# A four-layer decoder trunk: longer runs of equally wide matmuls, and attention scores with both low terms of a head in one product

## The chip, the cores and the metric

The kernel runs on one core of a Trainium2 chip. The metric is the device time of one execution in microseconds. In the profile PE is the matrix engine (TensorE) and PEld its weight loads, DVE is VectorE, ACT is ScalarE, POOL is GpSimd and SP is the engine that issues most transfers.

## The reference

The trunk has four layers over one stream h of 256 tokens with 1024 features, all in float32. Layers 0 and 3 mix tokens with differential attention, layer 1 with MoBA attention (one block of 256 at this length, so plain causal attention), layer 2 with sliding-window attention with sinks. After each mixer comes a squared-ReLU MLP with 4096 hidden features.

```python
for i in range(DEPTH):
    a = rms_norm(h, attn_norm_g[i])
    y = ...                      # by i % 3: diff_attention, moba_attention, swa_sink_attention
    h = h + y
    h = h + sqrelu_mlp(rms_norm(h, mlp_norm_g[i]), mlp_w_up[i], mlp_w_down[i])
return rms_norm(h, final_norm_g)

# in each mixer: q and k get a partial rotary turn, then
s = jnp.einsum('bqhcd,bkhcd->bhcqk', qi, k)      # diff: two components c for each of 8 heads
p = softmax(where(causal, s, -inf)); p = p[:, :, 0] - lam * p[:, :, 1]
o = jnp.einsum('bhqk,bkhe->bqhe', p, v)

def sqrelu_mlp(h, w_up, w_down):
    a = jnp.maximum(h @ w_up, 0)
    return (a * a) @ w_down
```

A head of queries or keys is 64 wide.

## The kernel before

**Two parts of each operand.** Float32 operands of the large products are split in a high part, rounded to the type fp32r, and a low part, the rest. A product is the sum of three: high by high, high by low and low by high. Weights come in pieces of 128 x 2048 elements (1 MB): one transfer to `raw`, then ACT writes `whi` and DVE writes `wlo` as `raw - whi`, half a piece (1024 columns) at a time. There are four buffers of `raw` and three each of `whi` and `wlo`; PE's last product on a piece frees its buffers.

**Stages of a layer.** Input projection (`proj`, accumulator `p_in`), mixer, output projection (`out_proj`, `p_d`), up projection (`up_proj`, `p_up`, 16 groups g of one piece each), down projection (`down_proj`, `p_down`, 16 pieces: two, h = 0 and 1, for each of 8 blocks d; in the last layer `down_out` with `p_last`). The activations are stored as `[..., (high, low), 256]`, so in up and down a product with a high weight takes both parts at once (512 columns, `part` 0) and one with a low weight takes the high part alone (256 columns, `part` 1). `block_step` issues one such product. In `up_proj` the order before is: block b of 128 output features, then part, then the 8 steps k over features; runs of eight 512-wide and eight 256-wide products alternate. The first group runs k outermost, since the normed inputs (`hg`, class `Normed`) become ready one after another. In `down_proj` the order is part, then 16 steps k.

The result of a group of up goes through `joined` (ACT copies the second half to `cross`, DVE adds it to the first), `squared` (tile `u`), `high` and `low` (tile `uu`).

**Scores.** `turn` transposes the queries or keys of two blocks on PE into a bank (`p_qk`). A block is two heads of 64 that stand one above the other on the 128 rows. `Queries` writes high and low to a tile `qhl`; `put_keys` writes the high part of the keys to `kpadh` and the low part to `kpadl`. The key tiles have an extra axis h of two: for h = 0 only rows 0 to 63 are filled, for h = 1 only rows 64 to 127, and the other rows hold zeros (`Keys.clear`, memsets on POOL), so one product with all 128 rows gives both heads side by side. `scores` does for each of two row tiles t of 128 queries three products (`mm3`): 256 wide for t = 0 and 512 wide for t = 1. `least` (DVE), `exp` (ACT), the division, `turned` (transposes `p_t`) and the values' products (`p_av`) follow, then the transposes `p_o` in layers 0 and 3, and the tile `oo`, which `p_d` reads. The mixer of layers 0, 1 and 3 has four groups of two blocks, that of layer 2 has 8 blocks too.

**Order of the work.** Everything is a task of a `Plan` with an engine, a cost in microseconds, the tasks before it, and buffers that it takes. The plan is run through as a simulation with those costs, and each engine's instructions are then issued in the order of the simulated start times and kept in that order (class `Ordered`). PE has a main sequence of weight products, and the tasks of the attention are put between them as soon as their inputs are due. The plan reserves for a score block 1.05 us of PE. Some tasks have a second engine that the plan may choose. All instructions go through one helper, so the profile shows line 191 for nearly all of them; tiles tell them apart.

Of the kernel before, what the change touches and what calls it, by code (L numbers as in the profile page):

```python
# [18 lines left out]
P = 128  # L19
# [15 lines left out]
LESS = 2.0  # L35
WAY = 0.6
MARGIN = 56


def f(ap):  # L40
# [157 lines left out]
def trunk(ctx: ExitStack, tc: tile.TileContext, xT, gains, lams, swa_row, fng, weights, out):  # L198
# [44 lines left out]
    def pe(cost, do, after=(), rank=1, **kw):  # L243
        return add("PE", cost, do, after, lag=0.3, rank=rank, **kw)
# [339 lines left out]

    COLS = (slice(1, 1 + P), slice(1 + P, 1 + 3 * P))

    def scores(q, k, mask, sinks, sums_of, after, begin=None):

        st = {}

        def products():
            st["p"] = [bank("p_s0"), bank("p_s1", 1)]
            (qh, ql), (kh, kl) = q(), k()
            for t, n in ((0, P), (1, S)):
                o = st["p"][t][:, :2 * n].rearrange("p (h m) -> p h m", h=2)
                a = slice(P * t, P * t + P)
                mm3(o, qh[:, a], ql[:, a], kh[:, :, :n], kl[:, :, :n], True, True)

        first = pe(1.05, products, after, take={"wk": 2, "e": 1})
# [46 lines left out]

    class Keys:

        def __init__(self, after):
            self.tiles = []  # L650

            def clear():
                for x in range(2):
                    t = room(10 + x, [P, 2, 2, S], f"kpad{'hl'[x]}", F32R)
                    self.tiles.append(t)
                    for h in range(2):
                        G.memset(f(t[HD * (1 - h):HD * (1 - h) + HD, :, h, :]), 0.0)

            self.clear = add("POOL", 2.2, clear, after)

    def turn(src, n, after):

# [10 lines left out]

    class Queries:

        def __init__(self, src, after):
            p, a = turn(src, 2, after)
            self.both = None

            def high():  # L680
                self.both = room(plan.now.got["q"][0], [P, 2, 2, S], "qhl", F32R)
                A.activation(self.both[:, 0], p(), AF.Copy, scale=0.125)

            def low():
                V.scalar_tensor_tensor(self.both[:, 1], p(), 0.125, f(self.both[:, 0]), op0=OP.mult, op1=OP.subtract)

            self.hi = act(512, high, [a], take={"q": 1})
            self.lo = dve(512, low, [self.hi])
            give("wk", [self.lo], a)

        def of(self, b):
            return lambda: [self.both[:, x, b] for x in range(2)]

    def put_keys(keys, src, n, after):

        p, a = turn(src, n, [keys.clear, *after])
        halves = [slice(HD * h, HD * h + HD) for h in range(2)]

        def high():
            for h, s in enumerate(halves):  # L700
                A.activation(keys.tiles[0][s, :n, h, :], p()[s], AF.Copy)

        def low():
            for h, s in enumerate(halves):
                V.tensor_tensor(keys.tiles[1][s, :n, h, :], p()[s], f(keys.tiles[0][s, :n, h, :]), op=OP.subtract)
# [4 lines left out]
        return lo  # L710

    class Diff:

# [3 lines left out]
        def head(self, h, q, k, after):  # L717
# [7 lines left out]
            st, exps, first = scores(q, k, causal, None, lambda c: l1[0] if c else self.l0[g][:, h % 2], after, begin)  # L725

            def combine():
                c2 = tiny.tile([P, NT], F32, tag="c2", name="c2")
# [84 lines left out]
    class Heads:  # L813
# [4 lines left out]
        def head(self, b, q, k, after):  # L818
# [2 lines left out]
            def begin():  # L821
                st2["l"] = tiny.tile([P, 2, NT], F32, tag="l", name="l", bufs=6)

            st, exps, first = scores(q, k, self.mask, self.sinks and self.sinks(b), lambda c: st2["l"][:, c], after, begin)
            ends, a = [], None
            for c in range(2):

# [59 lines left out]
    def mixer_layer(i, n):  # L887
        mixer, slot = i % 3, i // 3
        r = n.factor(False) if i else None
        keys = Keys([main[0]])  # L890
        if mixer == 2:
            return windowed(n, r, keys)
        v, vr, qk, queries, firsts = [], [], {}, [], []
# [2 lines left out]
        for at, c in enumerate((0, 1, "v", 2, 3, "v")):  # L896
# [14 lines left out]
            if c == "v":  # L911
                v.append(to)
                vr.append(got)
            else:
                if i == 0 and at == 0:
                    made["rope"] = rotary_tables()
                    made["lam"] = lambdas(pieces[-1].hi[-1].after[0])
                a = roped(to, 8, [*got, made["rope"]])
                queries.append(Queries(lambda j, t, to=to: to[0][:, t, P * j:P * j + P], [a]))
                k = put_keys(keys, lambda j, t, to=to: to[0][:, t, P * (2 + j):P * (2 + j) + P], 2, [a, *firsts[-2:]])  # L920
                for b in range(2):
                    h = 2 * c + b
                    firsts.append(heads.head(h, queries[c].of(b), lambda b=b: [x[:, b] for x in keys.tiles],
                                             [queries[c].lo, k]))
# [8 lines left out]
    def windowed(n, r, keys):  # L933
# [24 lines left out]
        for c, (width, other, pairs) in enumerate(((512, S, (0,)), (256, 0, (1,)), (512, 0, (2, 3)))):  # L958
# [17 lines left out]
            if c == 0:  # L976
                k = put_keys(keys, lambda j, t: st[0][:, t, P:2 * P], 1, [a])
            for g in pairs:
                q = Queries(lambda j, t, c=c, at=other + S * (g - pairs[0]): st[c][:, t, at + P * j:at + P * j + P], [a])
                for b in range(2):  # L980
                    firsts.append(heads.head(2 * g + b, q.of(b), lambda: [x[:, 0] for x in keys.tiles],
                                             [q.lo, k, negated]))
# [5 lines left out]

    def block_step(p, w, x, part, start, stop):
        if part:  # L990
            matmul(p[:, :S], w, x[:, 0], False, stop)
        else:
            matmul(r3(2)(p), w, x, start, False)

    def joined(o, p, after):

# [41 lines left out]
    def up_proj(n, then):  # L1038

        us = []  # L1040
        for g in range(16):
            w = piece()
            st = {}
            order = [(b, part, k) for b in range(2) for part in range(2) for k in range(8)]
            if g == 0:
                order.sort(key=lambda x: x[2])
            for at, (b, part, k) in enumerate(order):

                def do(b=b, part=part, k=k, w=w, st=st):
                    if not st:  # L1050
                        st["p"] = two_banks("p_up")
                    block_step(st["p"][:, b], w.at(part, 8, k)[:, P * b:P * b + P], n.both[k // 2][:, k % 2], part,
                               k == 0, k == 7)
# [9 lines left out]
            a = joined(sum_to, lambda st=st: st["p"], [t])  # L1063
            give("acc", [a], begin)

            def squared(st=st):
                st["u"] = sb.tile([P, 512], F32, tag="u", name="u")
# [16 lines left out]
    def down_proj(us, n, row):  # L1084
# [20 lines left out]
        for d in range(8):  # L1105
            if d % 2 == 0:
                st = {}
            for h in range(2):
                w = piece()
                for part, k in ((part, k) for part in range(2) for k in range(16)):  # L1110

                    def do(d=d, h=h, k=k, part=part, w=w, st=st):
                        if not st:
                            st["p"] = two_banks("p_down")
                        block_step(st["p"][:, d % 2], w.at(part, 16, k), us[16 * h + k][1](), part,
                                   h + k == 0, h == 1 and k == 15)
# [244 lines left out]
```

## Time and profile before

| | |
|---|---|
| median of 3 runs | 1142.52 us (1142.29 to 1143.0) |
| the profiled execution | 1142.88 us, its span 1141.1 us |
| instructions | 16569 |
| PE busy | 1128.6 us (99%) |
| DVE / ACT / POOL busy | 814.4 / 650.1 / 42.3 us |
| mean granted clock of TensorE | 0.997 |

The page gives busy times by engine, then the span in 40 slices, the queues, the chain of work that ended last, and groups of instructions. A matmul's busy time in the groups is that of one instruction from start to its modelled end, and neighbours overlap; the cost of one in a stream is read from the distance between starts, or from a stretch of the chain divided by its count.

### The profile page before, as it was taken

The page shows a single profiled execution, that of the slowest core. Times are in us where ns is not written, and L with a number is a line of the kernel's source. Part 1 is how long each engine was busy: PE and PEld are TensorE (multiplying, and loading weights), DVE is VectorE, ACT ScalarE, POOL GpSimd, SP SyncE. Part 2 cuts the span into 40 slices and gives each one's busy share as a digit, 9 for nine tenths or more (in the row PEclk, how much of TensorE's full clock was granted, in tenths as well). Part 3 has the DMA queues.
Part 4 walks back from the last instruction along what each step waited for, and adds up shares of the span by engine and source line. Part 5 has one row for each costly group of instructions (what it writes and reads, how often), then busy time and mean ns, then how long its engine had stood idle before and what let it go on. Part 6 is the DMA issues. An engine that isn't in the chain of part 4 may idle for free.

```text
span 1141.1 us, 16569 instructions
## 1 busy us (share of the span) xinstructions
PE 1128.6 (99%) x6462; PEld 983.4 (86%) x6462; DVE 814.4 (71%) x1385; ACT 650.1 (57%) x1126; POOL 42.3 (4%) x71
## 2 busy tenths in 40 slices
PE   8999999999999999999999999999999999999997
PEld 7889888888888898888887888888888899888886
DVE  8887887656676779775568799775568777877453
ACT  7877655444487665554446775544446776555342
POOL 1000000000100000000011000000010000100000
PEclk9999999999999999999999999999999999999999
DMA  8544555555444455555554175555544445555541
GB/s 305 186 148 147 213 194 185 185 185 188 159 144 160 139 198 194 188 184 185 186 176 141 39 257 186 184 185 187 188 159 169 148 143 179 196 184 203 185 147 37
DMA packets 30031, 198.65 MB, mean 174 GB/s; under 512 B 3456, under 2 KB 4864, under 8 KB 6528
## 3 DMA queue, kind: packets, MB, share of 16 engines
q1 hardware_dynamic: 29664, 197.19, 50.0%
q8 instruction: 51, 0.84, 0.3%
q10 hardware_dynamic: 288, 0.39, 0.1%
q14 instruction: 28, 0.23, 0.1%
HBM read 196.52 MB, written 1.05 MB: 173 GB/s over the span
## 4 chain that ended last, share of the span: by engine, by line
PE 98%; DVE 1%; issue 0%; DMA 0%; ACT 0%; POOLq 0%; POOL 0%; DVEq 0%
PE p_up L191 31%; PE p_down L191 23%; PE p_in L191 20%; PE p_d L191 8%; PE p_last L191 7%; PE p_s L191 3%; PE p_av L191 2%; PE p_t L191 1%; PE p_qk L191 1%; PE p_o L191 0%; DVE qn L191 0%; DMA gn<-in_gains 0%; DVE turns L191 0%; PE p_res L191 0%; DVE an L191 0%
## 5 line engine op out<-in xcount | busy, mean ns | idle before, releaser
L191 DVE TENSOR_TENSOR wlo<-raw,whi 128x1024 fp32r<-128x1024 f32 (+1 forms) x374 | 443.5, 1218 | 207.8 <-ACT whi L191 194.5
L191 ACT ACTIVATE whi<-raw 128x1024 fp32r<-128x1024 f32 (+1 forms) x374 | 374.2, 1042 | 320.2 <-issue 102.0
L191 PE MATMUL p_up<-hg,whi 128*128 128x512 f32 x1024 | 263.2, 393 | 0.0
L191 PEld LDWEIGHTS p_up<-hg,whi 128*128 128x128 f32 x1024 | 184.7, 189 | 33.8
L191 PE MATMUL p_in<-whi,hg 128*128 128x512 f32 (+1 forms) x672 | 187.2, 391 | 1.6 <-DVE hg L191 1.4
L191 PE MATMUL p_down<-uu,whi 128*128 128x512 f32 x768 | 183.2, 391 | 0.0
L191 PEld LDWEIGHTS p_down<-uu,whi 128*128 128x128 f32 x768 | 141.1, 188 | 27.3
L191 PE MATMUL p_up<-hg,wlo 128*128 128x256 f32 x1024 | 151.9, 282 | 0.0
L191 PEld LDWEIGHTS p_up<-hg,wlo 128*128 128x128 f32 x1024 | 143.1, 190 | 9.4
L191 PEld LDWEIGHTS p_in<-whi,hg 128*128 128x128 f32 x672 | 121.9, 188 | 25.5 <-DVE hg L191 1.8
L191 PE MATMUL p_in<-wlo,hg 128*128 128x512 f32 (+1 forms) x336 | 105.8, 390 | 0.4 <-DVE wlo L191 0.4
L191 PEld LDWEIGHTS p_down<-uu,wlo 128*128 128x128 f32 x768 | 98.5, 191 | 3.7
L191 PE MATMUL p_down<-uu,wlo 128*128 128x256 f32 x768 | 99.6, 283 | 0.0
L191 PE MATMUL p_d<-oo,whi 128*128 128x256 f32 x512 | 96.3, 289 | 0.0
L191 PEld LDWEIGHTS p_d<-oo,whi 128*128 128x128 f32 x512 | 80.0, 192 | 1.3 <-issue 1.1
L191 PE MATMUL p_last<-whi,uu 128*128 128x512 f32 x256 | 78.9, 389 | 0.0
L191 PEld LDWEIGHTS p_in<-wlo,hg 128*128 128x128 f32 x336 | 62.0, 188 | 13.0 <-DVE wlo L191 0.8
L191 PE MATMUL p_d<-oo,wlo 128*128 128x256 f32 x256 | 72.6, 284 | 0.0
L191 ACT ACTIVATE e<-ns,nm 128x128 f32<-128x128 f32 (+3 forms) x128 | 57.0, 449 | 14.8 <-DVE nm L191 14.1
L191 PEld LDWEIGHTS p_last<-whi,uu 128*128 128x128 f32 x256 | 48.1, 188 | 9.9
L191 ACT ACTIVATE uu<-u 128x512 fp32r<-128x512 f32 x64 | 40.0, 625 | 27.8 <-DVE u L191 27.8
L191 DVE TENSOR_TENSOR relu<-p_up,cross 128x512 f32<-128x512 f32 x64 | 43.9, 686 | 10.7 <-ACT cross L191 10.7
(155 smaller groups left out, 1000.6 us busy)
## 6 DMA issues: line engine op xcount, KB each, us to landing
raw<-in_weights SPq DMA_DIRECT2D x183, 1024.0 KB, 4.9
raw<-in_weights SPq DMA_DIRECT2D x8, 256.0 KB, 4.7
hT<-in_xT SPq DMA_DIRECT2D x8, 128.0 KB, 4.5
out<-last SPq DMA_DIRECT2D x2, 320.0 KB, 2.3
bias<-in_swa_row SPq DMA_DIRECT2D x1, 512.0 KB, 5.8
grow<-in_fng SPq DMA_DIRECT2D x1, 512.0 KB, 3.7
out<-last ACTq DMA_DIRECT2D x2, 192.0 KB, 2.3
lv<-in_lams SPq DMA_DIRECT2D x1, 256.0 KB, 7.8
```

The source lines that it names most:

```text
L191: x = getattr(self.engine, name)(*args, **kw)
```

## The change

Two things are changed.

1. Order in the MLP. `up_proj` runs both blocks b of a part before it changes the part, even groups with part 0 first and odd groups with part 1 first; the first group goes by two halves of four steps k. `down_proj` runs the second piece of each block d with part 1 first. The flags that start and end an accumulation follow. The tile `u` becomes two tiles, `u0` and `u1`, used in turn.

2. Scores of layers 0, 1 and 3 (`both` is true). The product of high queries and high keys stays as it is. For the two low terms, there is one tile for the queries (`qhl`) that holds, for head c, the low queries on the rows of head c and the high queries on the other 64 rows, and one tile for the keys (`kboth`) that holds for head c the high keys on the rows of head c and the low keys on the other rows. One product over 128 rows, for one head, then gives low by high and high by low at once: 128 or 256 columns wide, and two of them (c = 0, 1) for a row tile. The high queries now stand in a tile in the slots of `u0` and `u1`. The high parts on the other rows are copies between halves of the rows: a task `copied` of two instructions, with ACT as its engine and POOL as its second. The low queries are written in two halves. The zeros of the second key tile go. In layer 2 (`both` is false) the three products stay. In all four layers row tile 1 now comes before row tile 0. The plan reserves 0.82 us for the new block, 0.44 + 0.00164 n for a copy on ACT and 0.4 + 0.0024 n on POOL (n is 512, so 1.28 and 1.63).

```diff
-            for t, n in ((0, P), (1, S)):
+            for t, n in ((1, S), (0, P)):
                 o = st["p"][t][:, :2 * n].rearrange("p (h m) -> p h m", h=2)
                 a = slice(P * t, P * t + P)
-                mm3(o, qh[:, a], ql[:, a], kh[:, :, :n], kl[:, :, :n], True, True)
-
-        first = pe(1.05, products, after, take={"wk": 2, "e": 1})
+                if both:
+                    matmul(o, qh[:, a], kh[:, :, :n], True, False)
+                    for c in range(2):
+                        matmul(o[:, c], ql[:, c, a], kl[:, c, :n], False, True)
+                else:
+                    mm3(o, qh[:, a], ql[:, a], kh[:, :, :n], kl[:, :, :n], True, True)
+
+        first = pe(0.82 if both else 1.05, products, after, take={"wk": 2, "e": 1})
...
+                for t in self.tiles[:2 - both]:
+                    for h, s in enumerate(HALVES):
+                        G.memset(f(t[s, :, 1 - h, :]), 0.0)
+
+            self.clear = add("POOL", 2.2 - 1.1 * both, clear, after)
...
+    def copied(n, do, after):
+        t = add("ACT", 0.44 + 0.00164 * n, lambda: do(lambda o, x: A.activation(o, x, AF.Copy)), after)
+        t.ways["POOL"] = COPY * (0.4 + 0.0024 * n), lambda: do(G.tensor_copy)
+        return t
...
+                self.high = sb.tile([P, 2, S], F32R, tag=f"u{j - 2}", name="qh", bufs=1)
+                self.both = room(j, [P, 2, 2, S], "qhl", F32R)
+                A.activation(self.high, p(), AF.Copy, scale=0.125)
...
+                for h, s in enumerate(HALVES):
+                    V.scalar_tensor_tensor(self.both[s, :, h], p()[s], 0.125, f(self.high[s]), op0=OP.mult, op1=OP.subtract)
+
+            def beside(copy):
+                for h, s in enumerate(HALVES):
+                    copy(self.both[HALVES[1 - h], :, h], f(self.high[s]))
...
+            lo = dve(1024 if both else 512, low, [self.hi], 1 + both)
+            give("wk", [lo], a)
+            self.ready = [lo, copied(512, beside, [self.hi])] if both else [lo]
...
+                o = keys.tiles[1][HALVES[1 - h] if keys.both else s, :n, h, :]
+                V.tensor_tensor(o, p()[s], f(keys.tiles[0][s, :n, h, :]), op=OP.subtract)
+
+        def beside(copy):
+            for h, s in enumerate(HALVES):
+                copy(keys.tiles[1][s, :n, h, :], f(keys.tiles[0][s, :n, h, :]))
...
-            order = [(b, part, k) for b in range(2) for part in range(2) for k in range(8)]
+            turn = (0, 1) if g % 2 == 0 else (1, 0)
+            order = [(b, part, k) for part in turn for b in range(2) for k in range(8)]
             if g == 0:
-                order.sort(key=lambda x: x[2])
+                order = [(b, part, 4 * q + k) for q in range(2) for part in turn for k in range(4) for b in range(2)]
...
-                for part, k in ((part, k) for part in range(2) for k in range(16)):
+                for part, k in ((part, k) for part in ((0, 1), (1, 0))[h] for k in range(16)):
```

More of the change, by code (lines that the diff above doesn't have):

```diff
@@ L37 @@
 MARGIN = 56
+COPY = 1.0
 def f(ap):
@@ L585, in trunk, with scores @@
     COLS = (slice(1, 1 + P), slice(1 + P, 1 + 3 * P))
-    def scores(q, k, mask, sinks, sums_of, after, begin=None):
+    def scores(q, k, both, mask, sinks, sums_of, after, begin=None):
         st = {}
@@ L647, in trunk, with __init__ @@
     class Keys:
-        def __init__(self, after):
-            self.tiles = []
+        def __init__(self, both, after):
+            self.tiles, self.both = [], both
             def clear():
                 for x in range(2):
[L654 to L659, printed above, removed]
+                    self.tiles.append(room(10 + x, [P, 2, 2, S], ("kpad", "kboth")[x], F32R))
+                for t in self.tiles[:2 - both]:
+                    for h, s in enumerate(HALVES):
+                        G.memset(f(t[s, :, 1 - h, :]), 0.0)
+            self.clear = add("POOL", 2.2 - 1.1 * both, clear, after)
+    HALVES = [slice(HD * h, HD * h + HD) for h in range(2)]
+    def copied(n, do, after):
+        t = add("ACT", 0.44 + 0.00164 * n, lambda: do(lambda o, x: A.activation(o, x, AF.Copy)), after)
+        t.ways["POOL"] = COPY * (0.4 + 0.0024 * n), lambda: do(G.tensor_copy)
+        return t
     def turn(src, n, after):
@@ L674, in trunk, with __init__ @@
     class Queries:
-        def __init__(self, src, after):
+        def __init__(self, both, src, after):
             p, a = turn(src, 2, after)
-            self.both = None
             def high():
-                self.both = room(plan.now.got["q"][0], [P, 2, 2, S], "qhl", F32R)
-                A.activation(self.both[:, 0], p(), AF.Copy, scale=0.125)
+                j = plan.now.got["q"][0]
+                self.high = sb.tile([P, 2, S], F32R, tag=f"u{j - 2}", name="qh", bufs=1)
+                self.both = room(j, [P, 2, 2, S], "qhl", F32R)
+                A.activation(self.high, p(), AF.Copy, scale=0.125)
@@ L684, in low @@
             def low():
-                V.scalar_tensor_tensor(self.both[:, 1], p(), 0.125, f(self.both[:, 0]), op0=OP.mult, op1=OP.subtract)
+                if not both:
+                    V.scalar_tensor_tensor(self.both[:, 0], p(), 0.125, f(self.high), op0=OP.mult, op1=OP.subtract)
+                    return
+                for h, s in enumerate(HALVES):
[3 more added lines that the diff above has]
+                    copy(self.both[HALVES[1 - h], :, h], f(self.high[s]))
@@ L687, in __init__ @@
             self.hi = act(512, high, [a], take={"q": 1})
[L688 to L692, printed above, removed]
+            lo = dve(1024 if both else 512, low, [self.hi], 1 + both)
+            give("wk", [lo], a)
+            self.ready = [lo, copied(512, beside, [self.hi])] if both else [lo]
+            self.of = lambda b: lambda: (self.high[:, b], self.both[:, b] if both else self.both[:, 0, b])
@@ L694, in put_keys @@
     def put_keys(keys, src, n, after):
         p, a = turn(src, n, [keys.clear, *after])
-        halves = [slice(HD * h, HD * h + HD) for h in range(2)]
         def high():
-            for h, s in enumerate(halves):
+            for h, s in enumerate(HALVES):
                 A.activation(keys.tiles[0][s, :n, h, :], p()[s], AF.Copy)
         def low():
-            for h, s in enumerate(halves):
-                V.tensor_tensor(keys.tiles[1][s, :n, h, :], p()[s], f(keys.tiles[0][s, :n, h, :]), op=OP.subtract)
+            for h, s in enumerate(HALVES):
+                o = keys.tiles[1][HALVES[1 - h] if keys.both else s, :n, h, :]
+                V.tensor_tensor(o, p()[s], f(keys.tiles[0][s, :n, h, :]), op=OP.subtract)
@@ L707, in put_keys @@
+        def beside(copy):
+            for h, s in enumerate(HALVES):
+                copy(keys.tiles[1][s, :n, h, :], f(keys.tiles[0][s, :n, h, :]))
         hi = add("ACT", 0.36 + 0.00164 * S * n, high, [a])
@@ L709, in put_keys @@
         give("wk", [lo], a)
-        return lo
+        return [lo, copied(S * n, beside, [hi])] if keys.both else [lo]
     class Diff:
@@ L723, in begin @@
                 l1[0] = tiny.tile([P, NT], F32, tag="l", name="l", bufs=6)
-            st, exps, first = scores(q, k, causal, None, lambda c: l1[0] if c else self.l0[g][:, h % 2], after, begin)
+            st, exps, first = scores(q, k, True, causal, None, lambda c: l1[0] if c else self.l0[g][:, h % 2], after, begin)
             def combine():
@@ L822, in begin @@
                 st2["l"] = tiny.tile([P, 2, NT], F32, tag="l", name="l", bufs=6)
-            st, exps, first = scores(q, k, self.mask, self.sinks and self.sinks(b), lambda c: st2["l"][:, c], after, begin)
+            st, exps, first = scores(q, k, not self.sinks, self.mask, self.sinks and self.sinks(b), lambda c: st2["l"][:, c], after, begin)
             ends, a = [], None
@@ L889, in mixer_layer @@
         r = n.factor(False) if i else None
-        keys = Keys([main[0]])
+        keys = Keys(mixer != 2, [main[0]])
         if mixer == 2:
@@ L918, in mixer_layer @@
                 a = roped(to, 8, [*got, made["rope"]])
-                queries.append(Queries(lambda j, t, to=to: to[0][:, t, P * j:P * j + P], [a]))
+                queries.append(Queries(True, lambda j, t, to=to: to[0][:, t, P * j:P * j + P], [a]))
                 k = put_keys(keys, lambda j, t, to=to: to[0][:, t, P * (2 + j):P * (2 + j) + P], 2, [a, *firsts[-2:]])
@@ L923, in mixer_layer @@
                     firsts.append(heads.head(h, queries[c].of(b), lambda b=b: [x[:, b] for x in keys.tiles],
-                                             [queries[c].lo, k]))
+                                             [*queries[c].ready, *k]))
                 give("q", firsts[-2:], queries[c].hi)
@@ L978, in windowed @@
             for g in pairs:
-                q = Queries(lambda j, t, c=c, at=other + S * (g - pairs[0]): st[c][:, t, at + P * j:at + P * j + P], [a])
+                q = Queries(False, lambda j, t, c=c, at=other + S * (g - pairs[0]): st[c][:, t, at + P * j:at + P * j + P], [a])
                 for b in range(2):
                     firsts.append(heads.head(2 * g + b, q.of(b), lambda: [x[:, 0] for x in keys.tiles],
-                                             [q.lo, k, negated]))
+                                             [*q.ready, *k, negated]))
                 give("q", firsts[-2:], q.hi)
@@ L990, in block_step @@
         if part:
-            matmul(p[:, :S], w, x[:, 0], False, stop)
+            matmul(p[:, :S], w, x[:, 0], start, stop)
         else:
-            matmul(r3(2)(p), w, x, start, False)
+            matmul(r3(2)(p), w, x, start, stop)
     def joined(o, p, after):
@@ L1043, in up_proj, with do @@
             st = {}
-            order = [(b, part, k) for b in range(2) for part in range(2) for k in range(8)]
+            turn = (0, 1) if g % 2 == 0 else (1, 0)
+            order = [(b, part, k) for part in turn for b in range(2) for k in range(8)]
             if g == 0:
-                order.sort(key=lambda x: x[2])
+                order = [(b, part, 4 * q + k) for q in range(2) for part in turn for k in range(4) for b in range(2)]
             for at, (b, part, k) in enumerate(order):
-                def do(b=b, part=part, k=k, w=w, st=st):
+                def do(b=b, part=part, k=k, w=w, st=st, turn=turn):
                     if not st:
@@ L1052, in do @@
                     block_step(st["p"][:, b], w.at(part, 8, k)[:, P * b:P * b + P], n.both[k // 2][:, k % 2], part,
-                               k == 0, k == 7)
+                               k == 0 and part == turn[0], k == 7 and part == turn[1])
                 t = product(STEPS[part], do, [n.lo[k], w.ready(part, 8, k)], {"acc": 1} if at == 0 else None)
@@ L1064, in up_proj, with squared @@
             give("acc", [a], begin)
-            def squared(st=st):
-                st["u"] = sb.tile([P, 512], F32, tag="u", name="u")
+            def squared(st=st, g=g):
+                st["u"] = sb.tile([P, 512], F32, tag=f"u{g % 2}", name="u", bufs=1)
                 V.scalar_tensor_tensor(st["u"], st["t"], 0.0, st["t"], op0=OP.max, op1=OP.mult)
@@ L1115, in do @@
                         block_step(st["p"][:, d % 2], w.at(part, 16, k), us[16 * h + k][1](), part,
-                                   h + k == 0, h == 1 and k == 15)
+                                   h + k + part == 0, h == 1 and part == 0 and k == 15)
                     at = d % 2 + h + k + part
```

## The prediction

> **What bounds the kernel now.** I read the page's busy shares and chain first, then the waits of PE, then the chain in order of time, and last the timeline where the change touches it.
>
> ```profile
> span 1141.1 us, 16569 instructions
> PE 1128.6 (99%) x6462; PEld 983.4 (86%) x6462; DVE 814.4 (71%) x1385; ACT 650.1 (57%) x1126; POOL 42.3 (4%) x71
> PE 98%; DVE 1%; issue 0%; DMA 0%; ACT 0%; POOLq 0%; POOL 0%; DVEq 0%
> ```
> ```profile
> PE p_qk L191 <- DVE oo L191: 2.2, 1, 2.2
> PE p_in L191 <- DVE hg L191: 1.4, 1, 1.4
> PE p_warm L191 <- DVE minus_half L191: 1.1, 1, 1.1
> ```
>
> PE is busy nearly all the time, the chain that ends last is 98% PE, and its three largest waits sum to 4.7 us, one of them in the warm-up. So a microsecond of PE work that goes is a microsecond of the run, as long as nothing makes PE wait: PE's queue is in order, so a late operand holds every product behind it. The profiled execution took 1142.88 us (span 1141.1); the median of the three runs is 1142.52, 0.4 below. A measurement tells about 0.2%, or 2.3 us, from no change.
>
> The price of PE work comes from the chain in order of time (start, length, instructions):
>
> ```profile
> 37.19 2.10 PE p_s L191 x12
> 111.08 8.63 PE p_d L191 x72
> 119.71 89.47 PE p_up L191 x512
> 209.18 89.07 PE p_down L191 x512
> 1046.88 84.36 PE p_last L191 x372
> ```
>
> In p_last all products are 512 wide: 84.36/372 = 0.2268 us each. In that stretch of p_d all are 256 wide: 8.63/72 = 0.1199. An up or down stage has 256 products of each width: 256 x (0.2268 + 0.1199) = 88.75. Up takes 0.72 more, down 0.32 more. Down has 16 runs of 512-wide products, so a run costs 0.32/16 = 0.02 us on entering it. The timeline shows the run (start, length):
>
> ```profile
> 209.02 3.82 PE L191 MATMUL p_down<-uu,whi 128*128 128x512 f32 x16
> 212.67 2.08 PE L191 MATMUL p_down<-uu,wlo 128*128 128x256 f32 x16
> 214.58 3.82 PE L191 MATMUL p_down<-uu,whi 128*128 128x512 f32 x16
> ```
>
> Sixteen wide ones take 3.65 from start to start against 16 x 0.2268 = 3.63, and the sixteen narrow ones 1.91 against 1.92. Up has 30 runs of eight after its first group (0.60), and the first group, which changes width at every product, has the remaining 0.12.
>
> **Longer runs.** New order: the first group of up has two runs of 512, then low-high and high-low groups alternate, so groups 1+2, 3+4, ... 13+14 share a run (7), group 15 runs on into the first piece of down, down's pieces pair up (7 more), and the last piece of down runs into the 512-wide p_in. Runs entered per layer of the first three: 2 + 7 + 1 + 7 + 1 = 18, or 0.36 us. Before: 0.72 + 0.32 + 0.02 for p_in's own first run = 1.06. That is 0.70 saved, three times 2.1. In the last layer, which has p_last in place of down: 0.72 + 0.02 before, 2 + 7 + 1 = 10 runs after, 0.20; saved 0.54. **Sum: 2.6 us.** Bounds: nothing, if the loss is by count of products and not by changes of width (the down row, with the same product counts and 0.4 less, speaks against that), and 3.1 if a shared run costs nothing either.
>
> What could be late by the new order? A low-first group needs wlo at its start, not 1.8 us later. In these stages the split waits for free buffers:
>
> ```profile
> ACT whi L191 <- PE p_up L191: 91.6, 36, 3.1
> ACT whi L191 <- PE p_down L191: 69.8, 21, 3.6
> ```
>
> PE's last product on a piece frees its buffer, and with three of them the refilled one is used two pieces, 11 us, later. The first group of up now wants the eighth block of hg at 4.1 us after its start (8 x 0.2268 + 8 x 0.12 + 6 x 0.2268), before it was 4.9:
>
> ```profile
> 119.54 0.40 PE L191 MATMUL p_up<-hg,whi 128*128 128x512 f32 x1
> 121.20 1.68 DVE L191 SCALAR_TENSOR_TENSOR hg<-hT,gn,hg 128x256 fp32r<-128x256 f32 x4 [0.17 <-ACT hg L191]
> ```
>
> The last block lands at 122.88 and is wanted at 123.68. The fifth lands three steps of 0.4 earlier, at 121.68, and is wanted at 122.31. No wait, 0. In down, the second piece starts with low products, so the last block of uu is wanted 1.5 us earlier, at 214.58 + 1.7 = 216.3:
>
> ```profile
> 212.38 0.68 DVE L191 TENSOR_TENSOR uu<-u,uu 128x512 fp32r<-128x512 f32 x1
> ```
>
> It is done at 213.06: 0 again, with 3 us to spare.
>
> **Scores.** The chain's row of 2.10 us for 12 products is two heads: 1.05 each, of three 256-wide and three 512-wide products. There are 8 such blocks in each of the three layers, 24. After, a block has one 512-wide and two 256-wide products for the second row tile (0.2268 + 2 x 0.12 in place of 3 x 0.2268, a saving of 0.214), and one 256-wide and two 128-wide for the first (0.12 + 2x in place of 3 x 0.12, a saving of 2 x (0.12 - x)). The price x of a 128-wide product of this type (fp32r) stands nowhere in the trace. The nearest row is the values' product, plain f32 and 128 wide, two records for each product:
>
> ```profile
> 103.39 1.50 PE L191 MATMUL p_av<-v,et 128*128 128x128 f32 x12
> 104.64 0.48 PE L191 MATMUL p_d<-oo,whi 128*128 128x256 f32 x2
> 104.96 0.28 PE L191 MATMUL p_d<-oo,wlo 128*128 128x256 f32 x1
> 105.08 0.40 PE L191 MATMUL p_d<-oo,whi 128*128 128x256 f32 x2
> ```
>
> From 103.39 to 105.08 are these 12 records and three p_d products (0.36), so a record is (1.69 - 0.36)/12 = 0.111. Lower end: the line through 0.2268 at 512 and 0.1199 at 256 gives 0.067 at 128. Upper end: a whole plain f32 product, two records, 0.222. I take 0.111, one record of the same width with the same load of 128 weight columns. That load, too, leaves little room below:
>
> ```profile
> L191 PEld LDWEIGHTS p_av<-v,et 128*128 128x128 f32 x96 | 11.7, 191 | 0.4
> L191 PEld LDWEIGHTS p_av<-et,v 128*64 128x64 f32 x64 | 4.0, 136 | 2.1 <-issue 0.4 <-ACT e L191 0.4
> ```
>
> 64 columns more take 55 ns more, so 128 columns some 110 ns if loads follow one another. Saving per block 0.214 + 2 x 0.009 = 0.232, times 24: **5.6 us**. With x = 0.067 it is 7.7, with 0.222 it is 0.2. Each block enters a 512-wide run once, before and after. The Trainium skill, "TensorE: Matmul & The Clock Gate", section "Back-to-back issue gap", has a sustained 81 ns for 128 columns, by which this term would be 7.0 us; the same sentence has 131 ns for 512 columns, where this trace shows 226.8, so I do not lean on it.
>
> **What the scores add elsewhere.** Each of the 12 groups of two blocks gets one more DVE instruction (the low queries in two halves) and two copies of two instructions each, for queries and keys, on ACT or POOL:
>
> ```profile
> L191 DVE TENSOR_TENSOR kpadl<-p_qk,kpadh 64x512 fp32r<-64x512 f32 x24 | 16.5, 687 | 4.8 <-ACT kpadh L191 4.6
> L191 ACT ACTIVATE kpadh<-p_qk 64x512 fp32r<-64x512 f32 x24 | 14.1, 589 | 1.0 <-PE p_qk L191 0.8
> L191 POOL MEMSET kpadl<- 64x512 f32 x8 | 4.2, 522 | 0.4
> ```
>
> DVE: 12 x 0.69 = 8.2 us, 2.7 in a layer. A copy is two of the ACT rows, 1.18 us on ACT, 24 of them 28 us if all go there, 9.4 in a layer. On POOL a copy is at least two memsets, 1.04, against the 1.63 that the planner reserves. Room in the three mixer stages (window, length, busy of PE, PEld, DVE, ACT, POOL):
>
> ```profile
> 5.70:91.30 85.60, 83.84 (x416) 69.22 (x417) 73.70 (x204) 65.65 (x140) 2.57 (x3) 1.00 0.58 208
> 298.00:383.90 85.90, 85.90 (x448) 70.92 (x447) 63.59 (x166) 62.32 (x140) 3.16 (x4) 1.00 0.40 140
> 845.10:928.30 83.20, 83.20 (x420) 69.73 (x419) 67.14 (x172) 58.72 (x132) 5.17 (x6) 1.00 0.42 143
> ```
>
> DVE has 11.9 us free in the first of them and ACT 20, so both fit. What is not free is the order: the copies stand between the turn of queries and keys and the scores. The DVE half of that path is the longer one already:
>
> ```profile
> 35.08 1.39 DVE L191 TENSOR_TENSOR kpadl<-p_qk,kpadh 64x512 fp32r<-64x512 f32 x2 [0.40 <-ACT kpadh L191]
> 37.02 0.28 PE L191 MATMUL p_s<-kpadh,qhl 128*128 128x256 f32 x1
> ```
>
> The keys' low part is done at 36.47 and the scores start 0.55 later, and DVE's extra 0.69 makes that path later still; the planner puts other products ahead of the scores for it. POOL's pair, started with the last high part, ends about when DVE does. What the planner does not know is how long a copy on POOL waits when DVE is at its shared work. In the sliding-window layer the same tiny copy shows it:
>
> ```profile
> 614.27 0.19 POOL L191 COPY ns<-rest 128x2 f32<-128x2 f32 x1 [1.67 <-ACT e L191]
> 615.26 1.24 POOL L191 COPY ns<-rest 128x2 f32<-128x2 f32 x1 [0.81 <-ACT e L191]
> 615.25 1.20 DVE L191 TENSOR_TENSOR wlo<-raw,whi 128x1024 fp32r<-128x1024 f32 x1
> ```
>
> 0.19 us alone, 1.24 under a split's wlo, ending with it. wlo fills a third of the mixer stages (32.20 us of the first):
>
> ```profile
> 5.70:91.30 85.60, 30.61 (x96) 17.78 (x96) 32.20 (x31) 1.00 0.58 208
> ```
>
> A copy on POOL has 0.59 us in hand (1.63 - 1.04). One in three meets a wlo and loses 0.6 on average; half of those lose more than the margin, by some 0.3. That is 0.05 us a copy, 24 copies 1.2, less the share that goes to ACT: I take **0.9 us of PE waiting**. Bounds: 0, and (2 x 1.2 - 0.59) = 1.8 for each of 12 groups, 21.7. I stay near the low end because DVE, while it makes the low parts, runs no wlo. Halved memsets of the key tiles on POOL, the query tiles that move to u's slots and the scores' second bank first change nothing: POOL sits idle before the memsets, u is dead by then, and the next operation waits for the whole block.
>
> **Sum.** 2.6 + 5.6 - 0.9 = 7.3 us, from 1142.9 to 1135.6; against the median, 0.4 lower, about **1135.4**.
>
> **Rivals.** (1) A 128-wide product of this type costs as much as a plain one, 0.222. For it: no row shows one. Against it: every fp32r product here is one record (512 for the 512 products of down) where plain f32 is two. Time: 1142.5 - 2.6 - 0.2 + 0.9 = 1140.6, within or at the edge of no change; that is the change not doing what it says. (2) Collisions on POOL, the one that ends slower: each group's scores wait for a copy held up by wlo. It decides above 8.2/12 = 0.68 us a group, and at the full 1.8 the time is 1142.5 - 8.2 + 21.7 = 1156. For it: the 1.24 us copies. Against it: a hit needs a wlo in a window of some 1.5 us, and ACT can take the copy. The Trainium skill, "SBUF — State Buffer", section "Who interferes with whom", states this lock: a DVE instruction with two SBUF inputs and a GpSimd instruction that reads SBUF exclude each other, the later one blocked for the whole of the other. The rows just shown agree with it, and by it DVE's wlo can be held as well, some 0.5 us each time, which the free time of DVE takes up. (3) Low price and no waiting: x = 0.067, 1142.5 - 2.6 - 7.7 = 1132.2. (4) DVE, fuller by 2.7 us a layer, brings the last heads so much later, and p_d, which wants them, waits: half of it hidden 1142.5 - 8.2 + 4.1 = 1138.4, nothing hidden 1142.4. For it: DVE is 86% busy in the first mixer stage. Against it: PE waits for no head's product now but once, for 2.2 us, in the sliding-window layer.
>
> **How the numbers follow.** Forecast with 1133 to 1138.5: 0.57. Rival 1: 0.15. Rival 2: 0.09, most of it slower. Rival 3: 0.10. Rival 4: 0.09, half of it still faster by over 0.2% (under 1140.2). Range 1132.4 to 1141.0: from rival 3 to rival 1; left out are the worse parts of 2 and 4. Faster: 0.57 + 0.10 + 0.05 + a third of rival 1 (0.05) = 0.77; same: 0.15; slower: 0.08.
>
> **What would show it.** Up near 88.95 and down near 88.9 us in the chain, in place of 89.47 and 89.07; two score blocks in 1.64 us, not 2.10 (by rival 1 in 2.08); 128-wide p_s products spaced 0.11; PE's waits on score blocks, by POOL or ACT copies, under 2 us in all. POOL copies of 64x512 over 1 us each beside wlo, with PE waiting for them, would make me wrong, and so would new waits of p_d for oo.

## The result and the profile after

The changed kernel takes 1135.48 us (median of five runs, 1134.18 to 1136.83) against 1142.40 for the kernel before beside it, a ratio of 0.9941 (95% interval 0.9929 to 0.9952): 6.9 us less, where 7.3 was forecast. Timed again beside nine runs of the kernel before, with a median of 1140.82, it took 1135.44, ratio 0.9947 (0.9934 to 0.9959): 5.4 us less by the medians, 6.0 by the ratio. The forecast of 1135.4 holds, and so do its range and its direction; some of its reasons do not.

The page of the changed kernel, busy time by engine and share of the chain:

```profile
span 1133.7 us, 16638 instructions
PE 1120.9 (99%) x6462; PEld 982.5 (87%) x6462; DVE 819.3 (72%) x1396; ACT 663.5 (59%) x1149; POOL 53.4 (5%) x91
PE 97%; DVE 1%; ACT 0%; DMA 0%; issue 0%; SPq 0%; POOLq 0%; POOL 0%; ACTq 0%
```

PE is still busy 99% of the time, and its busy time fell by 7.7 us with the span's 7.4. The number of products is the same, 6462 records. So they became cheaper, and nothing took their place as the bound. The granted clock, the share of TensorE's full clock that the profile shows as granted, stands at half for 3.41 us in layer 2 and again after p_last, and it does so in both profiles alike, so the spans can be compared. The chain in order of time (start, length, count) shows where the time went, first before, then after:

```profile
410.79 89.47 PE p_up L191 x512
500.27 89.07 PE p_down L191 x512
666.74 89.47 PE p_up L191 x512
845.28 15.22 PE p_in L191 x67
```
```profile
118.95 88.95 PE p_up L192 x512
207.90 88.91 PE p_down L192 x512
316.52 1.57 PE p_s L192 x12
407.46 88.95 PE p_up L192 x512
496.42 88.91 PE p_down L192 x512
662.40 88.95 PE p_up L192 x512
751.36 88.91 PE p_down L192 x512
1039.50 84.33 PE p_last L192 x372
```

Every up stage of the first three layers lost 0.52 us and every down stage 0.16. Two blocks of scores take 1.57 us in the chain, where they took 2.10. A mixer with both projections lies between the end of a down stage and the start of the next up: 407.46 - 296.81 = 110.65 in layer 1, where it was 410.79 - 298.25 = 112.54, and 662.40 - 585.33 = 77.07 in layer 2 (before 77.40). From the start of the last layer to its p_last it is 199.23, before 201.60, of which up has about 0.5. The first up stage starts 0.76 earlier. The sum is 0.76 + 3 x 0.68 + 1.89 + 0.33 + 2.37 = 7.4, the whole difference of the spans.

PE's waits in the changed kernel after the warm-up (in all, times, longest):

```profile
PE p_qk L192 <- DVE qn L192: 2.5, 1, 2.5
PE p_in L192 <- DVE hg L192: 0.8, 1, 0.8
PE p_in L192 <- DVE wlo L192: 0.6, 1, 0.6
PE p_in L192 <- ACT qk L192: 0.5, 1, 0.5
PE p_d L192 <- ACT v L192: 0.2, 1, 0.2
```

No row has p_s: the scores wait for no copy. The two last rows are new, in layer 0; PE waits there for ACT to empty an accumulator of the input projection.

### The profile page after: what moved, and what is told of

Read it like the earlier page. It is cut to its first block, busy times and chain, and to the rows that moved or that the text cites. A ratio compares the mean times of both kernels' runs of the same rounds, so it can differ in the third digit from the quotient of the medians.

```text
span 1133.7 us, 16638 instructions
## 1 busy us (share of the span) xinstructions
PE 1120.9 (99%) x6462; PEld 982.5 (87%) x6462; DVE 819.3 (72%) x1396; ACT 663.5 (59%) x1149; POOL 53.4 (5%) x91
## 4 chain that ended last, share of the span: by engine, by line
PE 97%; DVE 1%; ACT 0%; DMA 0%; issue 0%; SPq 0%; POOLq 0%; POOL 0%; ACTq 0%
PE p_up L192 31%; PE p_down L192 24%; PE p_in L192 20%; PE p_d L192 8%; PE p_last L192 7%; PE p_s L192 2%; PE p_av L192 2%; PE p_t L192 1%; PE p_qk L192 1%; DMA raw<-in_weights 0%; PE p_o L192 0%; DVE wlo L192 0%; DVE qn L192 0%; PE p_res L192 0%; DVE kboth L192 0%
## 5 line engine op out<-in xcount | busy, mean ns | idle before, releaser
L192 PE MATMUL p_up<-hg,whi 128*128 128x512 f32 x1024 | 239.7, 390 | 0.0
L192 PEld LDWEIGHTS p_up<-hg,whi 128*128 128x128 f32 x1024 | 189.7, 188 | 37.7
L192 PE MATMUL p_down<-uu,whi 128*128 128x512 f32 x768 | 179.1, 390 | 0.0
L192 PEld LDWEIGHTS p_up<-hg,wlo 128*128 128x128 f32 x1024 | 127.6, 192 | 2.7
L192 PE MATMUL p_up<-hg,wlo 128*128 128x256 f32 x1024 | 128.8, 283 | 0.0
L192 PEld LDWEIGHTS p_down<-uu,wlo 128*128 128x128 f32 x768 | 95.3, 192 | 1.9
L192 PE MATMUL p_down<-uu,wlo 128*128 128x256 f32 x768 | 95.9, 283 | 0.0
L192 ACT ACTIVATE cross<-p_up 128x512 f32<-128x512 f32 x64 | 37.5, 587 | 47.9 <-PE p_up L192 47.9
L192 ACT ACTIVATE e<-ns,nm 128x128 f32<-128x128 f32 (+3 forms) x128 | 56.8, 448 | 11.7 <-DVE nm L192 11.2
```

What stands on the lines that cost most here:

```text
L192: x = getattr(self.engine, name)(*args, **kw)
```

## The experiments

**Theory**: PE's price alone made the gain: 0.02 us for each entered run of 512-wide products, and a score block cheaper by what its products cost. **Rivals**: the two parts need each other; the copies cost PE something on POOL or ACT; the toll belongs to the change of accumulator bank, not of width; 128-wide products are streamed at a lower price or as dear as plain f32.

### The order of the MLP alone

```diff
 # the kernel before, with
+            order = [(b, part, k) for part in turn for b in range(2) for k in range(8)]
+                for part, k in ((part, k) for part in ((0, 1), (1, 0))[h] for k in range(16)):
```

> The kernel before with the new order of products in the MLP alone; the scores stay three products. Theory (0.02 us for each entry of a 512-wide run after 256-wide products): up stages 88.95 us and down stages 88.91 in the chain, in place of 89.47 and 89.07, and 1142.4 - 2.5 = 1139.9. Rival (the order gains only together with the new scores, because it shifts work of DVE and ACT): stages shorter, but the time within 0.5 us of 1142.4.

It took 1139.69 us, ratio 0.9984 (0.9975 to 0.9992). Its chain:

```profile
119.22 88.95 PE p_up L191 x512
208.17 88.91 PE p_down L191 x512
409.61 88.95 PE p_up L191 x512
755.04 88.91 PE p_down L191 x512
1045.05 84.33 PE p_last L191 x372
```

The up and down stages are the forecast ones to 0.01 us, without the new scores. The order is worth 2.5 us in the stages and 0.9 to 2.9 in the timed ratio. The rival falls.

### The scores alone

```diff
 # the changed kernel, with
+            order = [(b, part, k) for b in range(2) for part in range(2) for k in range(8)]
+                for part, k in ((part, k) for part in range(2) for k in range(16)):
```

> The changed kernel with the MLP order of before. Theory (a block of scores 0.21 us cheaper on PE, 24 blocks, less 0.7 us of waits for ACT in the first layer): 1142.4 - 5.1 + 0.7 = 1138.0, and with the order-only run the two gains add up to the whole, 6.9. Rival (the copies cost PE more, and the order covers it): over 1139.5.

It took 1137.96 us, ratio 0.9965 (0.9953 to 0.9977), 4.0 us less. With the 1.8 of the ratio before it, the parts give 5.8, the whole 6.0 to 6.7 by its two ratios: they add up within their intervals. The span of its profile is 4.9 below that of before. The up and down stages are back at 89.47 and 89.07.

### Banks alternating, widths as in the changed kernel

```diff
-            order = [(b, part, k) for part in turn for b in range(2) for k in range(8)]
+            order = [(b, part, k) for part in turn for k in range(8) for b in range(2)]
```

> The changed kernel, with the two blocks b of an up group alternating at each product within a part: as many changes of width as in the changed kernel, but a change of accumulator bank at each product. Theory (the toll is for a change of width): up stages stay at 88.95 us. Rival (the toll of before was for the change of bank or block, which came with each change from 256 to 512): up stages 3 us and more above it, some 240 changes at 0.02.

```profile
118.90 88.95 PE p_up L192 x512
407.40 88.95 PE p_up L192 x512
```

The stages do not differ by 0.01 us from the changed kernel's. A change of bank at each product is free here, and the toll belongs to the width. Nor does it belong to the change from `whi` to `wlo`: p_last changes between them too, at one width, and takes 0.2268 a product throughout.

### Widths alternating

```diff
-            order = [(b, part, k) for part in turn for b in range(2) for k in range(8)]
+            order = [(b, part, k) for b in range(2) for k in range(8) for part in turn]
```

> The changed kernel, with 512- and 256-wide products alternating one by one in groups 1 to 15 of up. Theory (the toll builds up over the first five wide products of a run, 27 ns in all, less 7 ns on the first narrow ones, so a run of one pays only 6 to 7 ns): up stages 88.75 + 240 x 0.0067 = 90.4 us. Rival (0.02 us at each entry, however short the run): 88.75 + 240 x 0.02 = 93.6.

```profile
118.94 90.04 PE p_up L192 x512
408.56 89.85 PE p_up L192 x512
664.44 89.94 PE p_up L192 x512
```

The mean is 89.94, so (89.94 - 88.75 - 0.04 for the first group)/240 = 0.005 us for each pair, a little below the 0.0067 expected and a quarter of the 0.02 of a full run. The toll builds up over the first wide products of a run: in the up stages of the kernel before, the first five of the 120 runs of eight take on average 0.234, 0.236, 0.229, 0.233 and 0.231 us from start to start, the last three 0.227. Runs of one pay less for each change and, with 240 changes where the new order has about ten, more in all: 89.94, against 89.47 for runs of eight and 88.95 for the new order.

### The price of a 128-wide product

The changed kernel, with four more rounds of the pair for the first row tile:

```diff
                     for c in range(2):
-                        matmul(o[:, c], ql[:, c, a], kl[:, c, :n], False, True)
+                        matmul(o[:, c], ql[:, c, a], kl[:, c, :n], False, t == 1)
+                    for r in range(4 * (t == 0)):
+                        for c in range(2):
+                            matmul(o[:128, c], ql[:, c, a], kl[:, c, :n], False, r == 3)
```

> The changed kernel with each 128-wide product of the scores issued five times, which adds the low terms of the first row tile five times: 8 more in each of 24 blocks. Theory (0.115 us each, as the pair in the changed kernel costs with what it does to the next product): inner spacing 0.11 to 0.12 us and 0.92 us more for a block. Rival 1 (streaming alone, the 0.061 between the two is the price and the rest a one-time toll): spacing 0.061 to 0.067, 0.5 us more. Rival 2 (as dear as plain f32): 0.22, 1.8 us more.

One block from its timeline (start, length to the modelled end of the last, count):

```profile
324.38 0.39 PE L192 MATMUL p_s<-kpad,qh 128*128 128x512 f32 x1
324.61 0.40 PE L192 MATMUL p_s<-kboth,qhl 128*128 128x256 f32 x2
324.84 0.28 PE L192 MATMUL p_s<-kpad,qh 128*128 128x256 f32 x1
324.96 1.23 PE L192 MATMUL p_s<-kboth,qhl 128*128 128x128 f32 x10
326.02 0.45 PE L192 MATMUL p_s<-kpad,qh 128*128 128x512 f32 x1
```

The same block of the changed kernel has the pair alone, and so has the block behind it:

```profile
316.36 0.39 PE L192 MATMUL p_s<-kpad,qh 128*128 128x512 f32 x1
316.58 0.40 PE L192 MATMUL p_s<-kboth,qhl 128*128 128x256 f32 x2
316.81 0.28 PE L192 MATMUL p_s<-kpad,qh 128*128 128x256 f32 x1
316.93 0.34 PE L192 MATMUL p_s<-kboth,qhl 128*128 128x128 f32 x2
317.11 0.45 PE L192 MATMUL p_s<-kpad,qh 128*128 128x512 f32 x1
317.39 0.40 PE L192 MATMUL p_s<-kboth,qhl 128*128 128x256 f32 x2
```

Ten take 1.06 us from start to start, two take 0.18: eight more cost 0.88, 0.110 each. The theory's price and the forecast's row agree; 0.067 and 0.222 are out. That two take only 0.18 and not 0.22 is made up later: the 512-wide product behind them, at 317.11, is followed 0.28 later, where 0.23 is usual. Where 512-wide products of p_in stand behind a block, the first six take 0.08 us more than six times 0.2268 (the mean of nine places); before the change it was under 0.01.

### The same with half the weight columns

```diff
-                            matmul(o[:128, c], ql[:, c, a], kl[:, c, :n], False, r == 3)
+                            matmul(o[:64, c], ql[:, c, slice(0, 64)], kl[:, c, :n], False, r == 3)
```

> As the run before, but the 8 added products have weights of 64 query columns and fill 64 rows of the result alone. Theory (the price of a 128-wide product is the load of its 128 weight columns): spacing falls to between 0.055 and 0.07 us. Rival (it is a floor per product, or the moving side): spacing stays at that of the run before.

```profile
320.29 0.82 PE L192 MATMUL p_s<-kboth,qhl 128*128 128x128 f32 x10
320.94 0.44 PE L192 MATMUL p_s<-kpad,qh 128*128 128x512 f32 x1
```

Ten now take 0.65: eight more cost 0.47, 0.059 each. The moving side is the same 128 columns of keys; the weight columns were halved, and with them the rows of the result. So the price of a 128-wide product goes with its weight columns and not with its width; that it is their load, 0.11 us for 128, fits the 55 ns for 64 columns in the PEld rows of the prediction, but no run tells the load from the rows of the result. At 0.059 the product is also below the 0.067 of the line through the two wider ones. The Trainium skill, "TensorE: Matmul & The Clock Gate", section "LDWEIGHTS (loading the stationary operand)", gives a load as columns divided by 1.2, by estimate some 107 ns for 128; the 110 measured here agrees with it. The sustained 81 ns for 128 columns that the Trainium skill has on that page in the section "Back-to-back issue gap" are below what this stream reached.

### All copies on ACT

```diff
-        t.ways["POOL"] = COPY * (0.4 + 0.0024 * n), lambda: do(G.tensor_copy)
```

> The changed kernel with all 24 copies on ACT, none on POOL (in the changed kernel 13 of them ran on POOL). Theory (the copies have slack on either engine, and a copy on POOL that meets a split's wlo is not what PE waits for): ACT busy about 12 to 15 us more, time 1135 to 1136.5. Rival 1 (collisions on POOL cost PE): faster than 1134.5. Rival 2 (POOL was needed, ACT is on the path): over 1137.5.

It took 1136.27 us, ratio 0.9954 (0.9942 to 0.9966), within the theory's range but not for its reason; ACT's busy time grew by 9.2 us, less than the theory's 12 to 15. Its chain, its longest wait in layer 0, and two stretches of layer 0 (window, length, busy of PE, PEld, DVE, ACT, POOL, granted clock, DMA), first here, then in the changed kernel:

```profile
123.97 88.95 PE p_up L192 x512
664.87 88.95 PE p_up L192 x512
```
```profile
PE p_t L192 <- DVE e L192: 2.2, 1, 2.2
```
```profile
9.48:12.89 3.41, 3.41 (x8) 2.76 (x9) 3.41 (x9) 3.34 (x8) 0.00 (x0) 0.50 1.05 356
94.81:98.23 3.42, 3.42 (x18) 3.29 (x17) 2.92 (x14) 2.51 (x7) 0.00 (x0) 0.50 0.00 0
```
```profile
9.48:12.89 3.41, 3.41 (x15) 2.83 (x16) 3.41 (x10) 3.41 (x8) 0.00 (x0) 1.00 1.06 370
94.81:98.23 3.42, 3.42 (x32) 3.42 (x31) 2.73 (x13) 2.77 (x15) 0.00 (x0) 1.00 0.01 2
```

The first up stage starts 5.0 us later than in the changed kernel. PE's waits in layer 0 are 2.3 us longer, and twice the granted clock stood at half for 3.41 us, which it did not in layer 0 of the changed kernel: 8 products of p_in in place of 15 the first time, which is some 1.6 us at 0.2268 each, and up to 1.7, half the stretch, the second time (both are estimates). The mixer of layer 2, which has no copies, became 664.87 - 590.09 = 74.78, 2.3 shorter than 77.07; PE waits 1.1 us there in place of 2.5, and the stretch at half clock that the changed kernel has there (624.75 to 628.16) is missing. Without POOL as a way out the plan is another one in every layer, and the clock fell elsewhere, so this run isolates neither the price of a copy on ACT nor the worth of an order.

### The copies on POOL made twice

```diff
-        t.ways["POOL"] = ..., lambda: do(G.tensor_copy)
+        t.ways["POOL"] = ..., lambda: (do(G.tensor_copy), do(G.tensor_copy))
```

> The changed kernel with each copy on POOL written twice, by a plan that still reserves 1.63 us: a copy takes 2.67 us instead of 1.33. Theory (DVE's four low parts are what the scores wait for; POOL's copies end 1.8 us and more before the scores): no new wait of p_s on POOL, mixer stages within 0.5 us of the changed kernel's. Rival (the copies sit at the edge of the path, rival 2 of the prediction): waits of 0.5 us and more at each group with a copy on POOL, the mixer stages of layers 0, 1 and 3 together 5 us longer or more.

One run: 1136.61 us, span 1134.8, 1.1 above that of the changed kernel. It has one new wait:

```profile
PE p_s L192 <- POOL kboth L192: 1.0, 1, 1.0
```

It is in the one group of layer 1 that has both of its copies on POOL (that mixer is 1.2 longer, layer 3 the same to 0.01). Two more groups, in layers 0 and 3, have both on POOL and show no wait. So the theory holds but for one group, and the rival's 5 us did not come. The same group in the changed kernel, POOL then DVE:

```profile
325.45 1.82 POOL L192 CAST qhl<-qh 64x512 fp32r<-64x512 f32 x2 [10.96 <-ACT qh L192]
327.32 1.28 POOL L192 CAST kboth<-kpad 64x512 fp32r<-64x512 f32 x2
```
```profile
324.93 1.20 DVE L192 TENSOR_TENSOR wlo<-raw,whi 128x1024 fp32r<-128x1024 f32 x1
326.05 1.39 DVE L192 SCALAR_TENSOR_TENSOR qhl<-p_qk,qh 64x512 fp32r<-64x512 f32 x2
328.06 1.41 DVE L192 TENSOR_TENSOR kboth<-p_qk,kpad 64x512 fp32r<-64x512 f32 x2
```

The first copy is held by the split's wlo until about 326.05 (1.82 for the two, where two alone take 1.28). The collision is real. But the copies end at 328.60, DVE's low keys at 329.47, and the block starts at 331.65.

### The new scores in all four layers

```diff
-        keys = Keys(mixer != 2, [main[0]])
+        keys = Keys(True, [main[0]])
-            st, exps, first = scores(q, k, not self.sinks, self.mask, ...
+            st, exps, first = scores(q, k, True, self.mask, ...
-                q = Queries(False, ...
+                q = Queries(True, ...
```

> The new scores in the sliding-window layer too: 8 more blocks, 4 more copies of queries, one of keys, one memset pair fewer. Theory (PE price alone decides): 8 x 0.21 = 1.7 us less, 1133.8. Rival (that layer has PE waiting on DVE already, 2.5 us, and a longer path before the scores adds to it): 1135.0 to 1137, with a larger wait of p_qk or p_s.

1133.89 us, ratio 0.9927 (0.9915 to 0.9939), against 0.9941 and 0.9947 for the changed kernel. The mixer of layer 2 took 75.53 (661.94, the start of its up stage, less 586.41, the end of the down stage before), 1.54 less. PE's price decided again: PE still waits in that layer, 2.6 us in all against 2.5 in the changed kernel, 0.7 of it before p_qk. Layer 0 took 1.1 us longer, though all engines have the changed kernel's instructions there in the changed kernel's order. From 8.30 to 11.71 us its granted clock stood at half:

```profile
8.30:11.71 3.41, 3.17 (x7) 1.98 (x7) 3.34 (x10) 2.70 (x6) 0.00 (x0) 0.50 0.93 315
```

With the plan's reserve for POOL cut to what a copy takes:

```diff
-COPY = 1.0
+COPY = 0.82
```

> The new scores in all four layers, and the plan reserves 1.33 us for a copy on POOL (two instructions of 0.667 from start to start in the changed kernel) in place of 1.63. Theory (the copies are off the path, so the reserve decides nothing but the plan's order): within 1 us of the 1133.9 of the all-layers run, either way. Rival (a truer cost gives a better plan): under 1132.5.

1134.13 us, ratio 0.9937 (0.9925 to 0.9950): no gain, as the theory had it. With more passes of the plan:

```diff
-TRIES = 8
+TRIES = 24
```

> The new scores in all four layers, with 24 passes of the plan in place of 8, of which the shortest by its own reckoning is taken. Theory (what is left is start-up and the plan's luck in the mixer stages): 1132.5 to 1134; MLP stages the same to 0.02 us, mixer stages of layer 0 and 2 different by up to 2 us. Rival (PE has no waits left to gain): within 0.3 us of 1133.9.

```profile
118.92 88.95 PE p_up L192 x512
659.86 88.95 PE p_up L192 x512
8.30:11.71 3.41, 2.83 (x12) 2.01 (x12) 3.34 (x10) 3.24 (x7) 0.00 (x0) 1.00 0.99 316
```

1132.93 us (1132.34 to 1134.56), ratio 0.9930 (0.9916 to 0.9944). Beside it, on the same chip, the changed kernel was run once more:

> The changed kernel once more, beside the runs below: 1135.5, within 0.1% of its first timing against the kernel before.

It took 1135.44 (1134.65 to 1135.47), so the two do not overlap. The new scores in all four layers, 2.5 us below, beat both kernels. But the 24 passes found nothing: the trace has the same instructions in the same order on every engine as the run with 8. It is the same program timed again, and against that run the timed difference is within the intervals. The two profiles differ by 2.0 us all the same, and both steps lie where the clock was at half: 1.1 us by 11.7 us, where the row above shows it at full clock in this run, and 1.0 in layer 2 (659.86 - 585.30 = 74.56, against 75.53), where both have a stretch of 3.41 us, from 622.80 here and from 626.11 there, over other products. So the new scores in layer 2 gained 1.5 to 2.5 us, around the 1.7 of the theory.

## Why the prediction was right, and where not

- **Longer runs, 2.6 us.** Right to the stage: 88.95 and 88.91 were forecast and measured, 2.5 in all. The cause, the change of width, is shown by the alternating banks (nothing), by p_last and by the alternating widths.
- **No wait from the new order.** Right: no row for hg, uu or wlo in an MLP stage.
- **Price of a 128-wide product, 0.111 us from the nearest row.** Right: 0.110. It goes with the weight columns, as the two PEld rows suggested. Rival 1 (0.222) and rival 3 (0.067) fall.
- **Scores, 5.6 us.** Right in layers 1 and 3, where PE waits for nothing. The order-only run has the instruction order of before in its mixers; against it layer 1 went from 409.61 - 297.08 = 112.53 to 110.65, and the last layer up to p_last from 1045.05 - 843.95 = 201.10 to 199.23. That is 1.88 and 1.87, or 0.235 a block, where I had 0.232. It is paid in another place than I had it: "each block enters a 512-wide run once, before and after" took the two entries as equally dear, but the pair of 128-wide products takes 0.18 and not 0.22 itself, and the wide products behind it lose some 0.08 and not 0.02. In layer 1 the score products take 2.18 us less from start to start, and all other products together 0.30 more.
- **Waiting, 0.9 us.** The size was near, the mechanism wrong. The loss is in layer 0: its up stage starts 0.76 earlier than before and 0.27 earlier than in the order-only run, so 1.1 to 1.6 of the 1.88 are missing. The two new waits, for ACT's evictions of qk and v, are 0.7 of it; the rest is not traced. No score block waited for a copy. "POOL's pair, started with the last high part, ends about when DVE does" failed: in all ten groups with a copy on POOL it ends before DVE's low keys, and 1.8 us or more before the block starts. That is why the lock between DVE and POOL, which the profile after shows, cost nothing, and why rival 2 did not come, although a copy on POOL takes 1.28 and not 1.04, and four of the 26 instructions took more than 0.62, up to 1.16. Rival 4 did not come either: p_d waits for no oo.
- **Layer 2** was costed at nothing and is 0.33 shorter in the profile. Its order changed, by the row tiles and by the plan, but the clock alone moves that layer by more: in the order-only run, with the order of before, it took 666.09 - 587.48 = 78.61 with 6.83 us at half clock (626.16 to 632.99), and before 77.40 with 3.41. So this part has no shown cause. That it made up for some of the larger loss in layer 0, so that 7.4 came out where 7.3 was forecast, is luck.

## What to carry to other kernels

In a kernel that PE bounds, price a change in products by start-to-start distances in long stretches of one kind, and check whether the neighbours pay: here a run of narrow products pushed 0.02 to 0.08 us onto the wide ones behind it. Halving a product from 256 to 128 columns saved only 0.01 us here, since 128 weight columns cost 0.11 by themselves; merging two terms into one product saves down to that price and no further. Where an order comes from a planner, an edit can redraw stages that it does not touch, as the run without POOL did in layer 2. So compare stage by stage, and before a difference goes to the edit, see whether the instruction order is the same and what clock was granted in that stretch: two profiles of one program differed by 2.0 us at the places where the clock was halved, as much as a layer of new scores is worth.

## What was not expected of the hardware

The granted clock was not constant within a run. The profile before has a stretch at half clock from 628.69 to 632.10 us, and every profile has one or two such stretches before p_last ends, of 3.41 us, or of 6.83 in the order-only run, at the start, in layer 0 or in layer 2. By estimate one of 3.41 costs up to 1.7 us, half its length, where PE is busy throughout: the one at the start of the four-layer run cost 1.1. The times of one kernel go with it. Of the 17 runs of the kernel before beside the first experiments, those with a mean granted clock of 0.998 or 0.999 took 1140.42 to 1141.77 us, and those with 0.996 or 0.997 took 1142.02 to 1143.75. What makes the clock fall is not shown by any run here. Up and down stages, which had the full clock, repeat to 0.01 us between profiles of one order.

Two results were named by the expectations and are still worth keeping: halving the weight columns nearly halved a 128-wide product (0.110 to 0.059 us) with the moving side unchanged, and a change of accumulator bank at each product cost nothing that 0.01 us shows, while a change of width did.
